# A decoder trunk on one core: the last matrix of a block ended half by half, and x transposed by VectorE and DMA

## The chip, the cores and the metric

One core of one Trainium2 chip runs the whole program in one launch. The metric is the device time of one execution in microseconds (us), and less is better. The kernel before takes 1875.56 us (median of three runs, 1875.54 to 1876.08).

The engines are named as in the profile: PE is TensorE (PEld its weight loads), DVE is VectorE, ACT is ScalarE, POOL is GpSimd, SP is SyncE, which here issues nearly all DMAs. Each engine runs its own instructions strictly in the order in which they stand.

## The reference

Four layers over 256 tokens of width 1024, all in float32. With `i` the layer and three kinds of mixer in turn:

```python
for i in range(DEPTH):                        # DEPTH = 4
    x = x + 0.5 * swiglu(rms_norm(x, norm_g[i, 0]), ffn_gate[i, 0], ffn_up[i, 0], ffn_down[i, 0])
    hn = rms_norm(x, norm_g[i, 1])
    mix = (short_conv_mixer, mla_mixer, spatial_gating_mixer)[i % 3](hn, ...)
    x = x + mix
    x = x + 0.5 * swiglu(rms_norm(x, norm_g[i, 2]), ffn_gate[i, 1], ffn_up[i, 1], ffn_down[i, 1])

def rms_norm(x, g):                           # per token
    return x * rsqrt(mean(x * x) + 1e-6) * g
def swiglu(x, w_gate, w_up, w_down):          # 1024 -> 2816 -> 1024
    return (silu(x @ w_gate) * (x @ w_up)) @ w_down
```

So there are twelve blocks in a row, three to a layer (feed-forward, mixer, feed-forward). Each one begins with the norm of x and a product that contracts over the 1024 columns of x, and ends with a product that is added to x. The mixers are a short gated convolution (layers 0 and 3), latent attention (MLA, layer 1) and a spatial gating (layer 2).

## The kernel before

**Tokens.** The 256 tokens are two tiles of 128, `x0` and `x1`, that stay on chip with the tokens in the partitions. Each goes through the twelve blocks in a stream of its own (`stream(t)`, a Python generator). A `yield` ends a *turn*; the loop at the end gives the two streams their turns alternately, and stream 0 starts four turns ahead (`LAG`). What a turn emits is appended to the engines' orders; nothing is reordered afterwards. `later(n, f)` puts work off by n turns, counted over both streams.

**Weights.** All weight matrices form one list of *units* of 1024 columns in all (two k-tiles of 512 columns, or one k-tile of 1024). SP loads a unit (512 KB) into one of six `raw` buffers, ACT rounds it to float32r (`whi`, line 102) and DVE forms the rest (`wlo`, line 109). Each unit is used by stream 0 and then, four units later, by stream 1. A left operand is split in the same way (`split`, lines 243 and 244), and `products` (lines 289, 290 and 292) makes three matmuls of a product: high by high, high by low, and, last, low by high. One turn of a large product is one unit, six matmuls of 512 columns.

**The end of a block.** `linear_rows` takes units of one k-tile with all 1024 columns and writes two PSUM banks, one for each half of the columns. Both halves end with the last k-tile. `residual` then adds both to x on DVE (lines 363 and 365), and ACT sums the squares of both halves (line 353).

**The start of a block.** `normed` transposes x, since the contraction needs the columns of x in the partitions: for each half four transposes by PE with an identity (line 251), a multiplication by the norm's gain on DVE that empties the PSUM bank (line 334), and the split. The factor of the norm is applied later, to the product. `linear` then makes one bank of 512 columns over all eight k-tiles.

**A transpose without PE is there already**, for the hidden activations of the feed-forward (`turned`): DVE transposes blocks of 32 by 32 (line 391), SP writes the tile to HBM (`turn`, line 265) and reads it back in another order with four DMAs (line 269), and ACT and DVE split what arrived (lines 275 and 276, `take`).

In the names below, h0 and h1 are the first and second half of the 1024 columns of x.

Of the kernel before, what the change touches and what calls it, by code (L numbers as in the profile page):

```python
# [24 lines left out]
P = 128  # L25
# [25 lines left out]
LAG = 4  # L51
SKEW = 2
# [10 lines left out]
class Weights:  # L63
    """The weight matrices as one stream of units in the order of their use."""
# [56 lines left out]
def trunk(ctx: ExitStack, tc: tile.TileContext, x, positions, norm_g, ffn_gate, ffn_up, ffn_down,  # L121
# [185 lines left out]
    def linear_rows(t, a, n_kt):  # L307
# [18 lines left out]
    def normed(t, i, which):  # L326
        """x * gain, transposed and split, and the factor of each token: the first turn ends before, one between."""
        g0 = (i * 3 + which) * NK
        a = []
        for h in range(2):  # L330
            yield
            tr = transposed([xs[t][:, (4 * h + k) * P : (4 * h + k + 1) * P] for k in range(4)])
            xg = slot([P, 4, P])
            nc.vector.tensor_tensor(out=xg, in0=tr, op=ALU.mult,  # L334
                                    in1=columns[0][:, g0 + 4 * h : g0 + 4 * h + 4].unsqueeze(2).broadcast_to([P, 4, P]))
            a.append(split(xg, [P, 4, P]))
        in_chain[t] = False
        yield
        r = factor(sums_of_x[t] or sum_x(t))
        sums_of_x[t] = None  # L340
        return a, r

    sums_of_x = [None] * NT

    def factor(sums):
        total = tiny(1, "total")
        nc.gpsimd.tensor_tensor(out=total, in0=sums[0], in1=sums[1], op=ALU.add)  # L347
        return power(total, EPS, 1.0 / D, 1, "rstd")
# [19 lines left out]

# [1 line left out]
    def plan_ffn(i, j):  # L370
        for c, w in FF_CHUNKS:
            for m in (ffn_gate, ffn_up):
                W.add(m[i, j], c, w, NK, UNIT // w)
        W.add(ffn_down[i, j], 0, D, DFF // P, 1)

    def ffn(t, i, j, _):
        a, r = yield from normed(t, i, 2 * j)
        hs = []
        for n, (c, w) in enumerate(FF_CHUNKS):
            gate = yield from linear(t, a, w, NK)  # L380
            sg = slot([P, w])
            nc.scalar.activation(sg, gate[:, :w], AF.Silu, scale=r)  # L382
            yield
            up = yield from linear(t, a, w, NK)
# [5 lines left out]
            nc.vector.scalar_tensor_tensor(out=h, in0=up[:, :w], scalar=r, in1=sg, op0=ALU.mult, op1=ALU.mult)  # L390
# [6 lines left out]
        ps = yield from linear_rows(t, lambda k: hs[k // 4], DFF // P)  # L397
        residual(t, ps, 0.5)

# [1 line left out]
    def plan_conv(ia):  # L401
        for j in range(2):
            for part in (1, 2, 0):
                W.add(conv_w_in[ia], part * D + j * 512, 512, NK, 2)
        W.add(conv_w_out[ia], 0, D, NK, 1)

    def conv(t, i, ia, shared):
        a, r = yield from normed(t, i, 1)
# [26 lines left out]
        for j in range(2):  # L435
            c = yield from linear(t, a, 512, NK)
            cs = slot([P, 512])
            nc.scalar.activation(cs, c, AF.Copy, scale=r)
            yield
            hp = yield from linear(t, a, 512, NK)  # L440
# [9 lines left out]
        ps = yield from linear_rows(t, lambda k: ms[k // 4], NK)  # L450
        residual(t, ps, 1.0)

# [31 lines left out]
    def spatial(t, i, ic, _):  # L484
        a, r = yield from normed(t, i, 1)
        vs, sums = [], []
        for j in range(2):
            v = yield from linear(t, a, 512, NK)
# [4 lines left out]
            yield  # L493
# [36 lines left out]
    def plan_mla(ib):  # L530
# [5 lines left out]
        W.add(mla_w_o[ib], 0, D, NK, 1)  # L536
# [4 lines left out]
    def prepare_rope():  # L541
        """cos and sin [128 tok, NT, 16] of positions * inv_freq, the angle reduced exactly."""
# [111 lines left out]
    def rope_into(dst, src, table, t, n):  # L654
        """dst, src [128, n, 32]: rotated, with the gain in the table."""
# [9 lines left out]
    def mla(t, i, ib, shared):  # L665
        a, r = yield from normed(t, i, 1)
# [26 lines left out]
        def head_squares(y, n, how):  # L693
            """The sums of squares of y[:, h, :n]."""
# [162 lines left out]
    def stream(t):  # L857
        for n, (kind, i, j) in enumerate(blocks):
# [4 lines left out]
            yield from kinds[kind][1](t, i, j, shareds[n])  # L863
        for h in range(2):
            cols = slice(h * D // 2, (h + 1) * D // 2)
            (nc.sync, nc.scalar)[h].dma_start(out=out[0, t * P : (t + 1) * P, cols], in_=xs[t][:, cols])
# [44 lines left out]
```

## Time and profile before

| what | value |
| --- | --- |
| time, median of three runs | 1875.56 us |
| span of the profiled execution, first to last instruction | 1873.2 us |
| what lies around the span (the difference of the two) | 2.4 us |
| PE busy | 1852.3 us, 99% of the span |
| DVE, ACT, POOL busy | 60%, 47%, 5% |
| mean granted TensorE clock | 0.996 of full speed |
| moved by DMA | 382 MB, 204 GB/s over the span |

The profile is of one execution, and the page gives its span. Busy time of PE counts an instruction from its start to its modelled end, and neighbours overlap; what a matmul takes of PE's time is read from the distance between the starts of two in a row. Idle time with a releaser in brackets says what an instruction waited for.

### The profile page before, as it was taken

The numbers are of one execution on the slowest core, as the hardware profiler recorded it, in microseconds if no ns is written. First come the engines' busy times: TensorE is split into PE (matmuls) and PEld (weight loads), VectorE is DVE, ScalarE is ACT, GpSimd is POOL, SyncE is SP. The second block draws the span as 40 slices with busy tenths as digits, with TensorE's granted clock in tenths as the row PEclk, the third lists the DMA queues.
The fourth block names the chain that finished last, engine by engine and source line by source line (L and its number), as shares of the span: only waits on it lengthen the run. The fifth ranks groups of instructions, "written<-read, shape, count | busy, mean of one in ns | idle before, by whom it ended". The sixth has DMA issues, their size and how long they took to land.

```text
span 1873.2 us, 23300 instructions
## 1 busy us (share of the span) xinstructions
PE 1852.3 (99%) x8654; PEld 1523.4 (81%) x8654; DVE 1119.3 (60%) x1357; ACT 879.4 (47%) x1172; POOL 88.8 (5%) x222
## 2 busy tenths in 40 slices
PE   8999999999999989999999999999999999999998
PEld 6888888888888878888888888788888888888887
DVE  6555676565656476656556555565646564765662
ACT  5444454444445376544444445454435453544452
POOL 1000000000501031000010000000000000000000
PEclk9999999999999999999999999999999999999999
DMA  7777456777577630677757774467856784556782
GB/s 261 237 243 229 156 173 192 245 241 228 168 238 246 201 108 13 201 234 231 242 188 228 230 242 157 158 199 238 267 162 206 239 269 153 190 169 213 235 267 72
DMA packets 190162, 382.42 MB, mean 204 GB/s; under 512 B 14406, under 2 KB 57568, under 8 KB 190048
## 3 DMA queue, kind: packets, MB, share of 16 engines
q1 hardware_dynamic: 189040, 379.25, 63.0%
q0 software_dynamic: 608, 1.11, 0.2%
q8 instruction: 67, 1.10, 0.2%
q10 hardware_dynamic: 400, 0.57, 0.1%
q14 instruction: 47, 0.39, 0.1%
HBM read 356.76 MB, written 24.12 MB: 203 GB/s over the span
## 4 chain that ended last, share of the span: by engine, by line
PE 96%; ACT 2%; DVE 1%; issue 0%; DMA 0%; POOL 0%; SPq 0%; ACTq 0%; DVEq 0%
PE acc L289 31%; PE acc L292 31%; PE acc L290 31%; PE tr L251 2%; PE acc L820 1%; PE acc L793 1%; ACT whi L102 0%; DVE wlo L109 0%; DMA raw<-in_ffn_gate_dram 0%; ACT s L353 0%; ACT s L718 0%; ACT s L699 0%; ACT s L750 0%; PE acc L506 0%; DVE s L334 0%
## 5 line engine op out<-in xcount | busy, mean ns | idle before, releaser
L289 PE MATMUL acc<-whi,s 128*128 128x512 f32 (+2 forms) x2664 | 1028.3, 386 | 2.6 <-ACT s L243 1.8
L290 PE MATMUL acc<-wlo,s 128*128 128x512 f32 (+2 forms) x2664 | 1019.5, 383 | 1.6 <-DVE wlo L109 1.5
L292 PE MATMUL acc<-whi,s 128*128 128x512 f32 (+2 forms) x2664 | 953.6, 383 | 0.0
L109 DVE TENSOR_TENSOR wlo<-raw,whi 128x1024 fp32r<-128x1024 f32 (+1 forms) x634 | 749.8, 1214 | 182.2 <-ACT whi L102 181.0
L102 ACT ACTIVATE whi<-raw 128x1024 fp32r<-128x1024 f32 (+1 forms) x634 | 639.5, 1048 | 223.9 <-PE acc L292 202.3
L292 PEld LDWEIGHTS acc<-whi,s 128*128 128x128 f32 x2664 | 501.1, 188 | 106.6 <-DVE s L244 1.0
L289 PEld LDWEIGHTS acc<-whi,s 128*128 128x128 f32 x2664 | 501.3, 188 | 105.6 <-ACT s L243 2.9
L290 PEld LDWEIGHTS acc<-wlo,s 128*128 128x128 f32 x2664 | 501.6, 188 | 104.4 <-DVE wlo L109 2.5
L382 ACT ACTIVATE s<-acc,rstd 128x512 f32<-128x512 f32 (+1 forms) x96 | 62.7, 653 | 456.8 <-PE acc L292 447.9
L390 DVE SCALAR_TENSOR_TENSOR s<-acc,rstd,s 128x512 f32<-128x512 f32 (+1 forms) x96 | 67.7, 705 | 230.6 <-PE acc L292 230.1
L276 DVE TENSOR_TENSOR s<-big,s 128x512 fp32r<-128x512 f32 x96 | 61.8, 644 | 128.6 <-ACT s L275 128.6
L353 ACT ACTIVATE s<-x 128x512 bf16<-128x512 f32 x52 | 32.4, 623 | 110.8 <-DVE x L365 77.6
L243 ACT ACTIVATE s<-s 128x512 fp32r<-128x512 f32 (+1 forms) x58 | 36.4, 628 | 87.3 <-DVE s L334 63.8
L347 POOL TENSOR_TENSOR total<-ss,ss 128x1 f32<-128x1 f32 x26 | 6.3, 243 | 1446.6 <-ACT s L353 1446.6
L391 DVE STREAM_TRANSPOSE big<-s 128x512 f32<-128x512 f32 (+1 forms) x96 | 64.1, 667 | 3.3
L275 ACT ACTIVATE s<-big 128x512 fp32r<-128x512 f32 x96 | 56.2, 585 | 20.2 <-DMA big<-turn 19.9
L244 DVE TENSOR_TENSOR s<-s,s 128x512 fp32r<-128x512 f32 (+1 forms) x58 | 39.9, 688 | 40.3 <-ACT s L243 40.3
L365 DVE SCALAR_TENSOR_TENSOR x<-acc,x 128x512 f32<-128x512 f32 x32 | 20.6, 686 | 68.0 <-PE acc L292 68.0
L251 PE MATMUL tr<-ident,s 128*128 128x128 f32 (+1 forms) x222 | 33.6, 281 | 9.0 <-ACT s L765 2.5
L251 PEld LDWEIGHTS tr<-ident,s 128*128 128x128 f32 (+1 forms) x222 | 26.2, 140 | 16.5 <-ACT s L765 4.3
L334 DVE TENSOR_TENSOR s<-tr,columns 128x512 f32<-128x512 f32 x48 | 32.9, 686 | 8.8 <-PE tr L251 8.8
L251 PEld LDWEIGHTS tr<-ident,x 128*128 128x128 f32 x192 | 24.6, 144 | 6.1
(121 smaller groups left out, 412.4 us busy)
## 6 DMA issues: line engine op xcount, KB each, us to landing
raw<-in_ffn_gate_dram SPq DMA_DIRECT2D x176, 512.0 KB, 4.7
raw<-in_ffn_up_dram SPq DMA_DIRECT2D x176, 512.0 KB, 5.1
raw<-in_ffn_down_dram SPq DMA_DIRECT2D x176, 512.0 KB, 4.6
raw<-in_conv_w_in_dram SPq DMA_DIRECT2D x48, 512.0 KB, 3.9
turn<-big SPq DMA_DIRECT2D x32, 512.0 KB, 3.8
big<-turn SPq DMA_DIRECT2D x128, 128.0 KB, 4.5
raw<-in_conv_w_out_dram SPq DMA_DIRECT2D x16, 512.0 KB, 4.5
raw<-in_sg_w_in_dram SPq DMA_DIRECT2D x16, 512.0 KB, 3.7
```

What stands on the lines that cost most here:

```text
L102: nc.scalar.activation(hi, src, AF.Copy)
L109: self.nc.vector.tensor_tensor(out=lo, in0=src, in1=hi.bitcast(F32), op=ALU.subtract)
L244: nc.vector.tensor_tensor(out=lo, in0=src, in1=hi.bitcast(F32), op=ALU.subtract)
L251: nc.tensor.transpose(tr[: part.shape[-1], n, :], part, ident)
L275: nc.scalar.activation(hi.rearrange("p k (i b) -> p k i b", b=32), src, AF.Copy)
L276: nc.vector.tensor_tensor(out=lo.rearrange("p k (i b) -> p k i b", b=32), in0=src, in1=hi.bitcast(F32).rearrange("p k (i b) -> p k i b", b ...
L289: nc.tensor.matmul(ps, lhsT=ah[:, k, :], rhs=wh[:, wk, c], start=first, stop=False)
L290: nc.tensor.matmul(ps, lhsT=ah[:, k, :], rhs=wl[:, wk, c], start=False, stop=False)
L292: nc.tensor.matmul(ps, lhsT=al[:, k, :], rhs=wh[:, wk, c], start=False, stop=last)
L382: nc.scalar.activation(sg, gate[:, :w], AF.Silu, scale=r)
L390: nc.vector.scalar_tensor_tensor(out=h, in0=up[:, :w], scalar=r, in1=sg, op0=ALU.mult, op1=ALU.mult)
L391: nc.vector.transpose(z[:, :, k0 : k0 + w // P].rearrange("p j k b -> p k j b"), h.rearrange("p (k j b) -> p k j b", j=4, b=32))
```

## The change

- **A block's last product ends half by half.** Its last 8 k-tiles (feed-forward, `DOWN_TAIL`) or 4 (mixers, `OUT_TAIL`) are taken as units of two k-tiles and 512 columns: first all of h0, then all of h1 (`plan_rows`, `rows_into_x`). The residual of h0 is added four units (two in the mixers) before that of h1.
- **A block's first two products are interleaved by halves of k** (`plan_pair`, `linear_pair`): both over h0 of x first, then both over h1. This holds for gate and up, for two parts of the convolution's input matrix, and for two of spatial gating's.
- **Each half of x is transposed as soon as it is added, in one of two ways** (`prepare_x`). Where the block that begins is a mixer or the first feed-forward of a layer, `by_dma` holds: DVE transposes blocks of 32 by 32 (line 409), SP writes 256 KB to HBM (line 414) and reads it back with four DMAs (line 418), ACT multiplies by the gain in four pieces (line 423), and the split follows. Where it is the second feed-forward of a layer, the transposes stay on PE (`turn_by_pe`, line 433). With 12 blocks, 7 of the 11 passages from block to block go by DMA: 28 halves over the two streams.
- **The turns without work** at a block's start are two (four for MLA), before there were three that held the transposes.
- **The output** is stored half by half, without the sums of squares that no block needs.

```diff
+DOWN_TAIL, OUT_TAIL = 8, 4
+X_TURN, X_WRITE, X_READ, X_TAKE = 2, 1, 4, 8
+IDLE_FIRST, IDLE_DMA, IDLE_PE, IDLE_MLA = 1, 2, 2, 4
...
+    def plan_rows(w, n_kt, tail):
+        W.add(w, 0, D, n_kt - tail, 1)
+        for h in range(2):
+            W.add(w, 512 * h, 512, n_kt, 2, n_kt - tail)
+    def rows_into_x(t, a, n_kt, tail, factor, then):
+        ps = [acc(), acc()]
+        cols = [slice(0, 512), slice(512, 1024)]
+        for k in range(n_kt - tail):
+            products(ps, a(k), k % 4, unit(t), 0, cols, k == 0, False)
+            yield
+        for h in range(2):
+            for k in range(n_kt - tail, n_kt, 2):
+                w = unit(t)
+                for j in range(2):
+                    products([ps[h]], a(k + j), (k + j) % 4, w, j, [cols[0]], k + j == 0, k + j == n_kt - 1)
+                if k < n_kt - 2:
+                    yield
+            residual(t, ps[h], h, factor)
+            if then is not None:
+                prepare_x(t, h, *then)
+            else:
+                (nc.sync, nc.scalar)[h].dma_start(out=out[0, t * P : (t + 1) * P, 512 * h : 512 * h + 512], in_=x_half(t, h))
+            if h == 0:
                 yield
-        return ps
+        in_chain[t] = True
...
+    def linear_pair(t, a, width, n_kt, first_done):
+        ps = [acc(), acc()]
+        for k0 in range(0, n_kt, n_kt // 2):
+            for n in range(2):
+                k = k0
+                while k < k0 + n_kt // 2:
+                    w = unit(t)
+                    for j in range(w[2]):
+                        products([ps[n][:, :width]], a[(k + j) // 4], (k + j) % 4, w, j, [slice(0, width)], k + j == 0, k + j == n_kt - 1)
...
+    def prepare_x(t, h, i, which, by_dma):
+        g = gain_at(i, which, h)
+        lhs[t][h] = None
+        later(1, lambda: square_x(t, h))
+        if not by_dma:
+            later(X_TURN, lambda: turn_by_pe(t, h, g))
+            return
+        z = slot([P, 4, 4, 32])
+        nc.vector.transpose(z.rearrange("p j k b -> p k j b"), x_half(t, h).rearrange("p (k j b) -> p k j b", j=4, b=32))
+        d = dram.tile([4, 32, 4, 4, 32], F32, tag="xturn", name=name("xturn"))
+        y = slot([P, 4, 4, 32])
+        def write():
+            nc.sync.dma_start(out=d.rearrange("i a j k b -> (i a) j k b"), in_=z)
+        def read():
+            for j in range(4):
+                nc.sync.dma_start(out=y[32 * j : 32 * j + 32], in_=d[:, :, j].rearrange("i a k b -> a i k b"))
+        def take():
+            xg = slot([P, 4, P])
+            for k in range(4):
+                nc.scalar.activation(xg[:, k, :].rearrange("p (i b) -> p i b", b=32), y[:, :, k], AF.Copy, scale=g[:, k : k + 1])
+            lhs[t][h] = split(xg, [P, 4, P])
+        later(X_WRITE, write)
+        later(X_READ, read)
+        later(X_TAKE, take)
...
+    def normed(t, idle):
+        for _ in range(idle):
+            yield
+        in_chain[t] = False
+        return Lhs(t), factor(sums_of_x[t])
...
+                then = (next_i, 2 * next_j, n % 3 != 1) if next_kind == "ffn" else (next_i, 1, True)
```

The first place is DVE at the passage from the first feed-forward to the convolution. `x0_81` and `x1_82` are the two tiles of x. Before:

```order
L109 TENSOR_TENSOR wlo67_1607<-raw67_1508,whi67_1606 128x1024
L365 SCALAR_TENSOR_TENSOR x0_81<-acc_142_1191,x0_81 128x512
L365 SCALAR_TENSOR_TENSOR x0_81<-acc_143_1192,x0_81 128x512
L109 TENSOR_TENSOR wlo68_1625<-raw68_1526,whi68_1624 128x1024
L334 TENSOR_TENSOR s_168_1655<-tr_167_1650,columns0_87 128x512
L244 TENSOR_TENSOR s_170_1658<-s_168_1655,s_169_1657 128x512
```

And in the changed kernel, from h1's neighbours on (h0 of x0 was added and transposed six rows earlier). The first `L246` is the split of x0's h0 as it came back by DMA, the second that of x1's h0, the third that of x0's h1:

```order
L394 SCALAR_TENSOR_TENSOR x1_82<-acc_157_1290,x1_82 128x512
L409 STREAM_TRANSPOSE s_177_1638<-x1_82 128x4x4x32
L246 TENSOR_TENSOR s_185_1648<-s_183_1642,s_184_1647 128x512
L394 SCALAR_TENSOR_TENSOR x0_81<-acc_147_1192,x0_81 128x512
L409 STREAM_TRANSPOSE s_189_1665<-x0_81 128x4x4x32
L111 TENSOR_TENSOR wlo68_1656<-raw68_1526,whi68_1655 128x1024
L111 TENSOR_TENSOR wlo69_1706<-raw69_1544,whi69_1705 128x1024
L246 TENSOR_TENSOR s_205_1738<-s_203_1732,s_204_1737 128x512
L111 TENSOR_TENSOR wlo70_1724<-raw70_1571,whi70_1723 128x1024
L394 SCALAR_TENSOR_TENSOR x1_82<-acc_158_1291,x1_82 128x512
L409 STREAM_TRANSPOSE s_207_1751<-x1_82 128x4x4x32
L246 TENSOR_TENSOR s_215_1761<-s_213_1755,s_214_1760 128x512
```

The split of a half that came by DMA now stands ahead of the residual of the next half, and the third split stands behind a `wlo`, a residual and a transpose.

The second place is SP at the same passage. Before, it held only weight loads here:

```order
L89 DMA raw69_1544<-in_conv_w_in_dram 128x2x512
L89 DMA raw70_1562<-in_conv_w_in_dram 128x2x512
L89 DMA raw71_1580<-in_conv_w_in_dram 128x2x512
L89 DMA raw72_1598<-in_conv_w_in_dram 128x2x512
L89 DMA raw73_1616<-in_conv_w_in_dram 128x2x512
L89 DMA raw74_1642<-in_conv_w_in_dram 128x2x512
```

In the changed kernel (`xturn_169` is x0's h0, `xturn_178` x1's h0, `xturn_190` x0's h1):

```order
L414 DMA xturn_169_1564<-s_168_1562 128x512
L91 DMA raw70_1571<-in_conv_w_in_dram 128x2x512
L91 DMA raw71_1589<-in_conv_w_in_dram 128x2x512
L418 DMA s_170_1565<-xturn_169_1564 32x4x128 x4
L91 DMA raw72_1611<-in_conv_w_in_dram 128x2x512
L91 DMA raw73_1629<-in_conv_w_in_dram 128x2x512
L414 DMA xturn_178_1640<-s_177_1638 128x512
L414 DMA xturn_190_1667<-s_189_1665 128x512
L91 DMA raw74_1674<-in_conv_w_in_dram 128x2x512
L418 DMA s_179_1641<-xturn_178_1640 32x4x128 x4
L418 DMA s_191_1668<-xturn_190_1667 32x4x128 x4
```

Two weight loads stand between the write and the reads of x0's h0, and the reads of x1's h0 stand behind the write of x0's h1.

The third place is PE at the start of MLA, whose products are 416 columns wide. Before, `s_615` is the high part of x0's h0, and units of x1's last product (`acc_599`, `acc_600`) stand between its own:

```order
L289 MATMUL acc_624_5648<-whi230_5546,s_615_5615 128x416
L290 MATMUL acc_624_5648<-wlo230_5547,s_615_5615 128x416
L292 MATMUL acc_624_5648<-whi230_5546,s_616_5616 128x416
L289 MATMUL acc_624_5648<-whi230_5546,s_615_5615 128x416
L290 MATMUL acc_624_5648<-wlo230_5547,s_615_5615 128x416
L292 MATMUL acc_624_5648<-whi230_5546,s_616_5616 128x416
L289 MATMUL acc_599_5248<-whi229_5528,s_607_5389 128x512
L290 MATMUL acc_599_5248<-wlo229_5529,s_607_5389 128x512
L289 MATMUL acc_600_5249<-whi229_5528,s_607_5389 128x512
L290 MATMUL acc_600_5249<-wlo229_5529,s_607_5389 128x512
L292 MATMUL acc_599_5248<-whi229_5528,s_608_5390 128x512
L292 MATMUL acc_600_5249<-whi229_5528,s_608_5390 128x512
```

And now, with `s_686` the high part of x0's h0 and `s_710` that of x0's h1:

```order
L291 MATMUL acc_717_5755<-whi231_5633,s_686_5661 128x416
L292 MATMUL acc_717_5755<-wlo231_5634,s_686_5661 128x416
L294 MATMUL acc_717_5755<-whi231_5633,s_687_5662 128x416
L291 MATMUL acc_717_5755<-whi232_5669,s_710_5741 128x416
L292 MATMUL acc_717_5755<-wlo232_5670,s_710_5741 128x416
L294 MATMUL acc_717_5755<-whi232_5669,s_711_5742 128x416
```

Between the first product with h0 and the first with h1 stand 12 matmuls of x0 alone; before, units of x1's last product and PE's transposes stood among them.

## Rows read from the trace of the kernel before

**Rows 1.** The page: PE's and the others' busy time, GB/s in 40 slices, the chain.
```profile
PE 1852.3 (99%) x8654; PEld 1523.4 (81%) x8654; DVE 1119.3 (60%) x1357; ACT 879.4 (47%) x1172; POOL 88.8 (5%) x222
...
GB/s 261 237 243 229 156 173 192 245 241 228 168 238 246 201 108 13 201 234 231 242 188 228 230 242 157 158 199 238 267 162 206 239 269 153 190 169 213 235 267 72
...
PE 96%; ACT 2%; DVE 1%; issue 0%; DMA 0%; POOL 0%; SPq 0%; ACTq 0%; DVEq 0%
```

**Rows 2.** PE's groups: busy us, mean ns of one, idle before, releaser.
```profile
L251 PE MATMUL tr<-ident,x 128*128 128x128 f32 x192 | 29.5, 278 | 0.0
```

**Rows 3.** PE's timeline at a passage: start us, us, instruction.
```profile
193.98 0.60 PE L251 MATMUL tr<-ident,x 128*128 128x128 f32 x4
194.33 0.48 PE L289 MATMUL acc<-whi,s 128*128 128x512 f32 x1
194.65 0.39 PE L290 MATMUL acc<-wlo,s 128*128 128x512 f32 x1
...
195.81 0.60 PE L251 MATMUL tr<-ident,x 128*128 128x128 f32 x4
```

**Rows 4.** Groups of DVE and ACT by form, columns as in rows 2.
```profile
L365 DVE SCALAR_TENSOR_TENSOR x<-acc,x 128x512 f32<-128x512 f32 x32 | 20.6, 686 | 68.0 <-PE acc L292 68.0
L391 DVE STREAM_TRANSPOSE big<-s 128x512 f32<-128x512 f32 x80 | 56.9, 712 | 2.7
L244 DVE TENSOR_TENSOR s<-s,s 128x512 fp32r<-128x512 f32 x56 | 38.8, 693 | 39.1 <-ACT s L243 39.1
L109 DVE TENSOR_TENSOR wlo<-raw,whi 128x1024 fp32r<-128x1024 f32 x626 | 742.0, 1216 | 178.4 <-ACT whi L102 177.3 <-DMA turn<-big 0.3
...
L243 ACT ACTIVATE s<-s 128x512 fp32r<-128x512 f32 x56 | 35.4, 632 | 84.9 <-DVE s L334 63.8 <-DVE s L432 21.1
L353 ACT ACTIVATE s<-s 128x128 bf16<-128x128 f32 x2 | 0.6, 293 | 0.0
```

**Rows 5.** SP's and ACT's timeline: the third turned tile of the first feed-forward.
```profile
132.47 0.33 SPq L265 DMA_DIRECT2D turn<-big  x1
133.57 1.47 SPq L89 DMA_DIRECT2D raw<-in_ffn_down_dram  x2
135.09 1.85 SPq L269 DMA_DIRECT2D big<-turn  x4
...
143.27 0.63 ACT L275 ACTIVATE s<-big 128x512 fp32r<-128x512 f32 x1 [3.32 <-DMA big<-turn]
```

**Rows 6.** The same two engines: such a tile in two later feed-forwards.
```profile
1336.49 0.33 SPq L265 DMA_DIRECT2D turn<-big  x1
...
1345.17 0.63 ACT L275 ACTIVATE s<-big 128x512 fp32r<-128x512 f32 x1 [1.19 <-DMA big<-turn]
...
1802.40 0.33 SPq L265 DMA_DIRECT2D turn<-big  x1
...
1813.49 0.64 ACT L275 ACTIVATE s<-big 128x512 fp32r<-128x512 f32 x1 [3.61 <-DMA big<-turn]
```

**Rows 7.** DMA issues: count, KB each, median us from issue to landing.
```profile
out_dram<-x SPq DMA_DIRECT2D x2, 256.0 KB, 2.1
```

**Rows 8.** PE in MLA: timeline; then stretches (us, busy, clock, DMA share, GB/s).
```profile
671.33 0.35 PE L290 MATMUL acc<-wlo,s 128*128 128x416 f32 x1
671.52 0.35 PE L292 MATMUL acc<-whi,s 128*128 128x416 f32 x1
673.98 0.55 PE L251 MATMUL tr<-ident,s 128*128 128x128 f32 x3 [2.11 <-ACT s L669]
...
675.00:680.00 5.00, 4.70 (x23) 1.00 0.74 226
685.00:690.00 5.00, 5.00 (x27) 0.77 0.03 12
```

**Rows 9.** The whole timeline at the very end.
```profile
1868.17 1.29 DVE L365 SCALAR_TENSOR_TENSOR x<-acc,x 128x512 f32<-128x512 f32 x2 [4.25 <-PE acc L292]
...
1869.49 0.34 ACTq L866 DMA_DIRECT2D out_dram<-x  x1
```

More of the change, by code (lines that the diff above doesn't have):

```diff
@@ L324, in power @@
         return r
[L326 to L348, printed above, removed]
+    lhs = [[None, None] for _ in range(NT)]
+    sums_of_x = [[None, None] for _ in range(NT)]
     def square_sum(src):
@@ L370, in plan_ffn, with square_x, factor @@
[L370 to L377, printed above, removed]
+    def square_x(t, h):
+        sums_of_x[t][h] = square_sum(x_half(t, h))
+    def factor(sums):
+        total = tiny(1, "total")
+        nc.gpsimd.tensor_tensor(out=total, in0=sums[0], in1=sums[1], op=ALU.add)
+        return power(total, EPS, 1.0 / D, 1, "rstd")
@@ new lines, in x_half, with residual, gain_at @@
+    def x_half(t, h):
+        return xs[t][:, h * 512 : (h + 1) * 512]
+    def residual(t, ps, h, factor):
+        part = x_half(t, h)
+        if factor == 1.0:
+            nc.vector.tensor_tensor(out=part, in0=ps, in1=part, op=ALU.add)
+        else:
+            nc.vector.scalar_tensor_tensor(out=part, in0=ps, scalar=factor, in1=part, op0=ALU.mult, op1=ALU.add)
+    def gain_at(i, which, h):
+        g0 = (i * 3 + which) * NK + 4 * h
+        return columns[0][:, g0 : g0 + 4]
+    def prepare_x(t, h, i, which, by_dma):
[22 more added lines that the diff above has]
+        later(X_TAKE, take)
@@ new lines, in turn_by_pe, with __init__, __getitem__ @@
+    def turn_by_pe(t, h, g):
+        tr = transposed([xs[t][:, (4 * h + k) * P : (4 * h + k + 1) * P] for k in range(4)])
+        xg = slot([P, 4, P])
+        nc.vector.tensor_tensor(out=xg, in0=tr, op=ALU.mult, in1=g.unsqueeze(2).broadcast_to([P, 4, P]))
+        lhs[t][h] = split(xg, [P, 4, P])
+    class Lhs:
+        def __init__(self, t):
+            self.t = t
+        def __getitem__(self, h):
+            assert lhs[self.t][h] is not None, (self.t, h)
+            return lhs[self.t][h]
@@ L378, in ffn, with gate_done @@
+    def ffn(t, i, j, _, then):
+        a, r = yield from normed(t, IDLE_FIRST if i + j == 0 else (IDLE_DMA, IDLE_PE)[j])
         hs = []
+        sg = [None]
+        def gate_done(ps, w):
+            sg[0] = slot([P, w])
+            nc.scalar.activation(sg[0], ps[:, :w], AF.Silu, scale=r)
         for n, (c, w) in enumerate(FF_CHUNKS):
[L380 to L383, printed above, removed]
@@ L396, in ffn, with conv @@
             yield
-        ps = yield from linear_rows(t, lambda k: hs[k // 4], DFF // P)
-        residual(t, ps, 0.5)
+        yield from rows_into_x(t, lambda k: hs[k // 4], DFF // P, DOWN_TAIL, 0.5, then)
     def plan_conv(ia):
         for j in range(2):
-            for part in (1, 2, 0):
+            if j == 0:
+                plan_pair(conv_w_in[ia], conv_w_in[ia], D, 2 * D, 512, NK)
+            for part in (1, 2, 0)[2 - 2 * j :]:
                 W.add(conv_w_in[ia], part * D + j * 512, 512, NK, 2)
-        W.add(conv_w_out[ia], 0, D, NK, 1)
-    def conv(t, i, ia, shared):
-        a, r = yield from normed(t, i, 1)
+        plan_rows(conv_w_out[ia], NK, OUT_TAIL)
+    def conv(t, i, ia, shared, then):
+        a, r = yield from normed(t, IDLE_DMA)
         ms = [None] * 2
@@ L449, in conv @@
             yield
-        ps = yield from linear_rows(t, lambda k: ms[k // 4], NK)
-        residual(t, ps, 1.0)
+        yield from rows_into_x(t, lambda k: ms[k // 4], NK, OUT_TAIL, 1.0, then)
     def plan_spatial(ic):
-        for c in (D, D + 512, 0, 512):
+        plan_pair(sg_w_in[ic], sg_w_in[ic], D, D + 512, 512, NK)
+        for c in (0, 512):
             W.add(sg_w_in[ic], c, 512, NK, 2)
-        W.add(sg_w_out[ic], 0, D, NK, 1)
+        plan_rows(sg_w_out[ic], NK, OUT_TAIL)
     sg_wT = [fixed([P, 4, P], f"sg_wT{j}") for j in range(2)]
@@ L482, in prepare_spatial, with spatial, v_done @@
         later(70, load)
-    def spatial(t, i, ic, _):
-        a, r = yield from normed(t, i, 1)
+    def spatial(t, i, ic, _, then):
+        a, r = yield from normed(t, IDLE_DMA)
         vs, sums = [], []
-        for j in range(2):
-            v = yield from linear(t, a, 512, NK)
+        def v_done(v):
             vv = slot([P, 512])
@@ L525, in spatial @@
             yield
-        ps = yield from linear_rows(t, lambda k: ms[k // 4], NK)
-        residual(t, ps, 1.0)
+        yield from rows_into_x(t, lambda k: ms[k // 4], NK, OUT_TAIL, 1.0, then)
     def plan_mla(ib):
@@ L839, in mla @@
             yield
-        ps = yield from linear_rows(t, lambda k: os_[k // 4], NK)
-        residual(t, ps, 1.0)
+        yield from rows_into_x(t, lambda k: os_[k // 4], NK, OUT_TAIL, 1.0, then)
     kinds = {"ffn": (plan_ffn, ffn, None), "conv": (plan_conv, conv, None), "mla": (plan_mla, mla, prepare_mla),
@@ L857, in stream @@
     def stream(t):
+        for h in range(2):
+            yield
+            turn_by_pe(t, h, gain_at(0, 0, h))
+            later(1, lambda h=h: square_x(t, h))
         for n, (kind, i, j) in enumerate(blocks):
@@ L862, in stream @@
                     prepare(blocks[n + 1][2])
[L863 to L866, printed above, removed]
+            then = None
+            if n + 1 < len(blocks):
+                next_kind, next_i, next_j = blocks[n + 1]
+                then = (next_i, 2 * next_j, n % 3 != 1) if next_kind == "ffn" else (next_i, 1, True)
+            yield from kinds[kind][1](t, i, j, shareds[n], then)
     with tc.manual_schedule(engines=MANUAL):
```

65 lines of the change are left out of this document (38 added, 27 removed).

## The prediction

> **What bounds the kernel now.** The page first [rows 1]: PE is busy 99% of the span and makes 96% of the chain that ended last; DVE, ACT and the DMA engines have slack. So only what PE runs and what PE waits for counts. Then PE's groups [rows 2]: the 192 transposes of x never left PE idle, so the old start of a block hides its chain and there is nothing to win there but PE's own time. PE's timeline gives the prices [rows 3]: the last five matmuls of 512 columns of a unit take 1.16 us (194.65 to 195.81), 0.232 us each, so a unit of six takes 1.39 us. PE's longest waits, the 2.1 us at 673.98 among them, lie in MLA [rows 8].
>
> **PE loses transposes.** Four of them take 0.35 us (193.98 to 194.33), and the matmul behind them is followed after 0.32 instead of 0.23 us (194.33 to 194.65): 0.44 us for a group [rows 3]. 28 halves go by DMA now: 28 x 0.44 = 12.3 us less on PE, all of it on the path. The matmuls of the tails and the pairs are the same as before in number and width, so PE's other work is unchanged.
>
> **The end.** Now two residuals (1.29 us) stand between the last matmul and the last store [rows 9]; then one does. 0.6 us less.
>
> **The way by DMA, one half (x0's h0).** I count from the end of the last matmul of that half. DVE starts after 0.1 us; residual 0.69, transpose 0.71 [rows 4]: the write is issued at 1.5. For the DMAs the trace has the same pattern on SP, write, two weight loads, four reads: from 132.47 to 143.27 the third tile of the first feed-forward took 10.8 us until ACT, which stood waiting for it, could start [rows 5]. There are eight such tiles; they took 8.7 (the quickest) to 11.1 us, 9.8 in the mean [rows 6]. They hold 384 KB, x's half 256 KB: 0.25 MB less in all at some 240 GB/s [rows 1] is 1.0 us, so 8.8 us. The bounds: two transfers as quick as a lone store of 256 KB, 2.1 us each [rows 7], and 1.4 us to issue three reads ahead of the fourth [rows 5], 5.6 us; above, the slowest tile as it is, 11.1. I take 8.8, since the neighbours on the queue are the same. The data are there at 10.3. Then ACT's four pieces, 4 x 0.29 = 1.2, high part 0.63, low part 0.69 [rows 4]: high at 12.1, low at 12.8 (9.6 to 15.1).
>
> The Trainium skill prices this lower: "DMA: Bandwidth & Descriptors", section "Anatomy of one DMA", gives about 2.0 us for each DMA whatever its size, plus its bytes. By it an estimate for write and reads is 2.6 + 2.6 us and the issue of the reads, 6.6 us in all. The lone store of 256 KB at 2.1 us agrees with it [rows 7]; the loaded queue, with 8.7 to 11.1 us, does not [rows 6], and the trace decides. What it would give is the first rival.
>
> **What hides it.** PE reaches x0's h0 ten units later, at 13.9 us: hidden. But each engine works in its own order. On DVE the split of h0 stands ahead of the residual of x0's h1, whose last matmul ends at 11.1 (eight units). So that residual starts at 12.8 instead of 11.2, and the write of h1 is issued at 14.2. On SP the reads of x1's h0 stand behind that write: 1.1 us for the write, 0.4 for a load [rows 5], then two times four reads, 15.7 to 17.5 and 17.5 to 19.4. In rows 5 and 6 all reads had landed 5.2 to 8.5 us (mean 7.1) after the first was issued; here 0.6 MB less stands ahead, 2.3 us less: 4.8. So x1's h0 lands at 20.5, x0's h1 a quarter of a megabyte later, at 21.5. ACT splits the one (high at 22.3) and then the other (high at 24.1). DVE: low part of x1's h0 at 23.0, then `wlo` 1.22, the residual of x1's h1 and its transpose, 1.40, and only then the low part of x0's h1, at 26.3. PE wants x0's h1 nine units after its last matmul, at 23.6, and its low part two matmuls later, at 24.1. Stall: 2.2 us. With the quick bound the delay on DVE goes and the stall is 0; with the slow one it is about 4.5. x1's h1 has ten units and the stall before it: hidden. There are six such passages (two into the convolution, three into a layer's first feed-forward, one into spatial gating): 6 x 2.2 = 13.2 us, between 0 and 27.
>
> **MLA.** Here the first product is not a pair. x0's h0 is wanted after twelve units: hidden. x0's h1 is wanted 12 matmuls of 416 columns later, 0.19 us each [rows 8], at 16.7 + 2.3 = 19.0, its low part at 19.4. By the steps above its high part is there at 24.1, and the low one at 25.1 (no `wlo` stands before it here): 5.7 us of stall, 3.0 with the quick bound. x1's h1 is added on DVE at 23.7, written at 24.4, landed by 30.4 and split by 32.2 and 32.9, while PE, which resumed at 25.1, wants it at 29.7: 2.8 more. Before, PE stood 2.1 us at this place for the evacuation of x0's product [rows 8]; now units of x1 cover that: 2.1 back. x0's next split stands on ACT behind this `take`: some 1.5 us (between 0 and 3). 5.7 + 2.8 - 2.1 + 1.5 = 7.9 us, between 1 and 11.
>
> **Edits at nothing.** The four passages to a layer's second feed-forward keep PE's transposes one unit after the residual, as before, which cost PE no wait [rows 2]; if the residual came later than 1.39 us, PE would wait for the rest. ACT gets 28 x 1.2 = 33 us more, at 47% busy; where it blocks on a landing, `whi` made three units ahead covers it, and the price without that cover is the wait itself. SP blocks on a write's landing before its reads, as it does now for every turned tile; weights have six buffers ahead of it, 6 x 2 x 1.39 = 16.7 us, and if these ran out PE would wait for `whi`. 14.7 MB more on the queues is 4% of 382 MB. The paired products fill two banks instead of one for two units; six banks are there.
>
> **Sum.** The profiled execution's span is 1873.2 us, with 2.4 us around it that stay: the median, 1875.6. -12.3 - 0.6 + 13.2 + 7.9 = +8.2: 1883.8 us.
>
> **Rivals.** *All hidden but MLA.* If a half's DMAs take 7 us or less, the split of h0 is done when h1's last matmul is, nothing cascades, and the six passages cost 0. For it: a lone store takes 2.1 us [rows 7], and a half of x is smaller than any turned tile. Against it: eight waits for such reads out of eight, with the same neighbours on the queue [rows 5, 6]. With MLA at 4: -12.9 + 4 = 1866.7 us, faster. *Halfway.* DMAs a microsecond shorter than mine, stalls of 1 us: -12.9 + 6 + 6, 1874.7 us, no change. *The clock falls.* In MLA a wait of 2.1 us alone [rows 8] left the granted clock at 1.00 (675 to 680); after further waits it was 0.77 over 5 us (685 to 690), a mix of 2.4 and 1.2 GHz, which loses 1.15 us. If each of the seven passages brought that, 8 us more than the forecast: 1892 us. The place is the first units of a block, the price 1.15 us each, and it decides where two stalls come within a few units. The Trainium skill ("TensorE: Matmul & The Clock Gate", section "HAM oscillation — how this bites in real kernels") has this rule: waits for DMA between bursts of matmuls bring the clock to its lower level again and again. The trace has it for MLA only.
>
> **Chances.** Forecast, slower: 0.42 (0.05 of it so near that nothing can be told). All hidden: 0.33, of which 0.02 within the bound. Halfway: 0.15, of which 0.03 faster and 0.12 no change. The clock: 0.10, slower. A measurement of this kernel tells 0.2%, 3.75 us. So faster 0.34, no change 0.19, slower 0.47. The forecast's own range is 1877 to 1891 (stalls of 1 to 3.5 us in the six); with the cases of the other sign 1863 (nothing waits but MLA's three microseconds) to 1897 (stalls of 3.5 us and the clock).
>
> **What would show it.** PE's transposes of x: 80 instead of 192. In PE's idle time, some 2 us at the first product with x0's h1 in six passages, released by ACT or DVE line 246 (not by the weights), and 5 us or more in MLA. On DVE, line 394 for h1 held behind line 246 although PE is done; on ACT, line 423 waiting for `xturn`'s reads. Wrong would be: no wait of PE on line 246 outside MLA, or reads that land within 7 us of their write. If PE waits on `whi` or `wlo` instead, the queue on SP or a blocked ACT is the cost, which I put at nothing.

## The result: 1898.8 us, 1.3% slower

The changed kernel takes 1898.84 us (median of four runs, 1896.66 to 1905.40) against 1875.71; the ratio is 1.013, 95% interval [1.0112, 1.0147]. The forecast was slower, by 8.2 us; it became 23.1, 2 us above the top of the range. The profile is of the quickest of the four runs.

The page of the kernel after (its span is 1894.9 us), with the groups that answer to [rows 1, 2]:

```profile
PE 1851.4 (98%) x8542; PEld 1512.8 (80%) x8542; DVE 1118.0 (59%) x1357; ACT 908.4 (48%) x1276; POOL 114.7 (6%) x222
PE 88%; DMA 4%; ACT 3%; DVE 3%; SPq 1%; issue 1%; ACTq 0%; DVEq 0%
L291 PE MATMUL acc<-whi,s 128*128 128x512 f32 (+1 forms) x2664 | 1029.8, 387 | 20.2 <-ACT s L245 19.3
L294 PE MATMUL acc<-whi,s 128*128 128x512 f32 (+1 forms) x2664 | 982.0, 384 | 7.4 <-DVE s L246 7.3
L423 ACT ACTIVATE s<-s,columns 128x128 f32<-128x128 f32 x112 | 35.8, 390 | 94.0 <-DMA s<-xturn 94.0
...
L253 PE MATMUL tr<-ident,x 128*128 128x128 f32 x80 | 13.4, 297 | 0.0
```

80 transposes of x are left on PE instead of 192, as forecast. But PE's share of the chain that ended last fell from 96% to 88%, and DMA, ACT and DVE stand in it. PE waits 19.3 us for high parts of x (ACT, line 245) and 7.3 us for low parts (DVE, line 246).

The idle time in these two rows, 27.6 us, is not all that was lost: PE's busy time has hardly fallen (1852.3 to 1851.4) though 12.3 us of transposes are gone. PE's timeline at the passage from the first feed-forward into the convolution shows why (start, duration, idle before and releaser), beside [rows 3]:

```profile
202.98 0.39 PE L294 MATMUL acc<-whi,s 128*128 128x512 f32 x1
204.57 0.50 PE L291 MATMUL acc<-whi,s 128*128 128x512 f32 x1 [1.20 <-ACT s L245]
204.91 0.40 PE L292 MATMUL acc<-wlo,s 128*128 128x512 f32 x1
205.30 0.50 PE L294 MATMUL acc<-whi,s 128*128 128x512 f32 x1
205.64 0.40 PE L291 MATMUL acc<-whi,s 128*128 128x512 f32 x1
...
206.41 0.50 PE L291 MATMUL acc<-whi,s 128*128 128x512 f32 x1
206.74 0.40 PE L292 MATMUL acc<-wlo,s 128*128 128x512 f32 x1
208.35 0.50 PE L294 MATMUL acc<-whi,s 128*128 128x512 f32 x1 [1.21 <-DVE s L246]
208.69 0.39 PE L291 MATMUL acc<-whi,s 128*128 128x512 f32 x1
```

From 202.98 to 208.69 there are ten starts, which take 2.32 us at 0.232; they take 5.71, so 3.4 us are lost, and the brackets show 2.4. Matmuls overlap, so a wait begins to cost 0.16 us before it counts as idle; and a matmul that had to wait is followed after 0.34 instead of 0.23 us, which happens twice for a half, since its high part comes first and its low part just behind it (205.30). From here on losses are taken from starts. Summed so, the six passages lose 3.4, 3.3, 8.6, 3.7, 3.1 and 2.5 us: 24.5 in all, where the forecast had 13.2.

What PE waits for stands on the other three engines (the same passage, from the residual of x0's h0 on):

```profile
181.15 0.69 DVE L394 SCALAR_TENSOR_TENSOR x<-acc,x 128x512 f32<-128x512 f32 x1 [7.41 <-PE acc L294]
...
182.61 0.34 SPq L414 DMA_DIRECT2D xturn<-s  x1
...
185.31 1.84 SPq L418 DMA_DIRECT2D s<-xturn  x4
...
192.00 1.31 ACT L423 ACTIVATE s<-s,columns 128x128 f32<-128x128 f32 x4 [6.56 <-DMA s<-xturn]
192.36 4.06 SPq L414 DMA_DIRECT2D xturn<-s  x2
193.34 0.63 ACT L245 ACTIVATE s<-s 128x512 fp32r<-128x512 f32 x1
194.01 0.69 DVE L246 TENSOR_TENSOR s<-s,s 128x512 fp32r<-128x512 f32 x1 [1.67 <-ACT s L245]
194.62 0.68 DVE L394 SCALAR_TENSOR_TENSOR x<-acc,x 128x512 f32<-128x512 f32 x1
197.66 3.97 SPq L418 DMA_DIRECT2D s<-xturn  x8
202.58 1.28 ACT L423 ACTIVATE s<-s,columns 128x128 f32<-128x128 f32 x4 [4.53 <-DMA s<-xturn]
203.89 0.63 ACT L245 ACTIVATE s<-s 128x512 fp32r<-128x512 f32 x1
...
204.42 1.26 ACT L423 ACTIVATE s<-s,columns 128x128 f32<-128x128 f32 x4
...
205.72 0.63 ACT L245 ACTIVATE s<-s 128x512 fp32r<-128x512 f32 x1
206.30 0.68 DVE L394 SCALAR_TENSOR_TENSOR x<-acc,x 128x512 f32<-128x512 f32 x1
...
207.65 0.65 DVE L246 TENSOR_TENSOR s<-s,s 128x512 fp32r<-128x512 f32 x1
```

The residual of x0's h1 (194.62) follows the split of x0's h0 without a gap, 2.3 us after it could have run (the end of h0's last matmul is put at 181.05, 0.1 us ahead of its residual; that of h1 ends eight units, 11.1 us, later, and DVE follows after 0.1); its write on SP (the second of the two, done at 196.42) is as late; the eight reads for two halves then go out together, and ACT takes both halves back to back (202.58, 204.42). The low part of x0's h1 (207.65) stands behind a weight's low part, the residual of x1's h1 and its transpose.

### The profile page after: what moved, and what is told of

Same layout as the page of the kernel before. It is cut to its first block, busy times and chain, and to the rows that moved or that the text cites. A ratio compares the mean times of both kernels' runs of the same rounds, so it can differ in the third digit from the quotient of the medians.

```text
span 1894.9 us, 23349 instructions
## 1 busy us (share of the span) xinstructions
PE 1851.4 (98%) x8542; PEld 1512.8 (80%) x8542; DVE 1118.0 (59%) x1357; ACT 908.4 (48%) x1276; POOL 114.7 (6%) x222
## 4 chain that ended last, share of the span: by engine, by line
PE 88%; DMA 4%; ACT 3%; DVE 3%; SPq 1%; issue 1%; ACTq 0%; DVEq 0%
PE acc L294 28%; PE acc L291 28%; PE acc L292 28%; DMA s<-xturn 3%; PE tr L253 2%; DVE wlo L111 1%; ACT s L423 1%; SPq L418 1%; ACT s L245 1%; DVE s L246 1%; DMA xturn<-s 1%; PE acc L919 1%; PE acc L892 1%; DVE x L394 0%; ACT whi L104 0%
## 5 line engine op out<-in xcount | busy, mean ns | idle before, releaser
L291 PE MATMUL acc<-whi,s 128*128 128x512 f32 (+1 forms) x2664 | 1029.8, 387 | 20.2 <-ACT s L245 19.3
L292 PE MATMUL acc<-wlo,s 128*128 128x512 f32 (+1 forms) x2664 | 1022.2, 384 | 1.5 <-DVE wlo L111 1.5
L294 PE MATMUL acc<-whi,s 128*128 128x512 f32 (+1 forms) x2664 | 982.0, 384 | 7.4 <-DVE s L246 7.3
L246 DVE TENSOR_TENSOR s<-s,s 128x512 fp32r<-128x512 f32 (+1 forms) x58 | 39.6, 683 | 114.7 <-ACT s L245 114.7
L383 POOL TENSOR_TENSOR total<-ss,ss 128x1 f32<-128x1 f32 x26 | 14.1, 542 | 1449.5 <-ACT s L375 1449.5
L423 ACT ACTIVATE s<-s,columns 128x128 f32<-128x128 f32 x112 | 35.8, 390 | 94.0 <-DMA s<-xturn 94.0
L520 DVE SCALAR_TENSOR_TENSOR s<-s,columns,s 128x128 f32<-128x128 f32 x64 | 22.5, 352 | 2.3
```

## The experiments

Each ratio is to the kernel before, run beside the variant. A1 is the theory that what costs is not the transfer but what stands in order behind an instruction that waits for its landing.

**1. All halves by PE**, ends by halves and pairs kept:

```
-  then = (next_i, 2 * next_j, n % 3 != 1) if next_kind == "ffn" else (next_i, 1, True)
+  then = (next_i, 2 * next_j, False) if next_kind == "ffn" else (next_i, 1, False)
```

> The changed kernel with every half of x turned by PE again (192 transposes of x); the ends by column halves and the pairs stay. Theory A (the loss is PE waiting for the DMA-turned halves): nothing waits, and only the shorter end is left of the change, 1875 us (1873 to 1877), ratio to the kernel before about 1.000. Rival B (finishing by halves and pairing the first products costs PE time by itself, since PE's recorded busy time fell by 0.9 us where 12.3 us of transposes went): the 11 us stay, 1885 us or more.

Measured 1873.33 us, ratio 0.9988 [0.9979, 0.9997]. Rival B falls: the new order of products costs nothing and is worth some 1.8 us (0.6 to 3.9 by the interval). All the loss lies in the DMA way.

**2. The take one unit later.**

```
-X_TURN, X_WRITE, X_READ, X_TAKE = 2, 1, 4, 8
+X_TURN, X_WRITE, X_READ, X_TAKE = 2, 1, 4, 9
```

> The changed kernel with X_TAKE = 9 for 8: on DVE the residual of x0's h1 comes ahead of the split of x0's h0, which waits for a landing; all DMAs are the same. Theory A1 (the landing is late by a microsecond, and the queue on DVE passes that on): x0's h1 leaves 2.3 us earlier, x1's h0 and x0's h1 land as much earlier, the six passages lose 0 to 1 us instead of 3.4 and MLA some 4.5 instead of 7: 1880 us (1876 to 1884). Rival C (the DMA round trip itself is what PE waits for, whoever stands ahead on DVE): unchanged, 1896 to 1900 us, with 3 us of wait in each passage.

Measured 1886.79 us, 1.0058 [1.0043, 1.0073]. 12 us came back with the same DMAs in the program, so C falls as it stood; but A1 had hoped for 19, and the time lies 3 us above its window. PE's timeline, the first passage:

```profile
203.92 0.50 PE L291 MATMUL acc<-whi,s 128*128 128x512 f32 x1 [0.74 <-ACT s L245]
206.37 0.50 PE L291 MATMUL acc<-whi,s 128*128 128x512 f32 x1 [0.52 <-ACT s L245]
```

The wait for a low part is gone (in the changed kernel 1.21 at 208.35), that for x1's h0 is shorter (0.74 for 1.20), x0's h1 is now waited for at its high part (0.52), and each wait still brings its two slow restarts. MLA's wait fell only from 7.08 to 6.36. Of the 10.0 us between the two profiled executions 6.0 lie at the one passage behind the sixth block, which loses 2.6 instead of 8.6 us. The other five lose 14.1 us where they lost 15.9, so there most of what C said holds: ACT takes x1's h0 0.1 us after it has landed (201.82).

**3. MLA by PE.**

```
-  ... else (next_i, 1, True)
+  ... else (next_i, 1, next_kind != "mla")
```

> The changed kernel with the four halves into MLA turned by PE, the rest by DMA as they were. Theory A: MLA's entry costs 7.7 us of the difference; PE's 7 us wait at its first product goes, the 2 us wait of before for the evacuation may come back: 1891 us (1889 to 1893). Rival (the waits in MLA are covered by the later waits of that block, which would move up): 1896 us or more.

Measured 1888.92 us, 1.0072 [1.0056, 1.0089]: 9.9 us back by the medians, 8.2 between the profiled executions; the trace of the changed kernel has 7.2 for MLA (below).

**4. Both edits**, those of 2 and 3 together.

> X_TAKE = 9 and MLA's halves by PE. Theory A1: both savings add, 1874 us (1871 to 1878). Rival C: as the variant with MLA alone, 1889 to 1893 us.

Measured 1881.33 us, 1.0033 [1.0022, 1.0044]: 5.5 us under the second, 7.6 under the third. That misses A1's window by 3 us, and so does not beat PE's transposes: a passage saves 4 x 0.44 = 1.8 us and loses 2.9 in the mean (2.6 in the first one, where 0.9 shows as idle). A half that comes just in time is still too late.

**5 to 8. A longer tail**, so that h0 ends 5.6 us earlier (two units of its own stream and two of the other's). It stands on top of the fourth; then on top of the second, with h0 alone by DMA (the second pair of lines); on top of the third; and on top of the first.

```
-DOWN_TAIL, OUT_TAIL = 8, 4
+DOWN_TAIL, OUT_TAIL = 12, 4
...
-        if not by_dma:
+        if h == 1 or not by_dma:
```

> The variant with X_TAKE = 9 and MLA's halves by PE, and DOWN_TAIL = 12 for 8: the first column half ends six units before the stream's end instead of four, so x0's h0 and x1's h0 have 5.6 us more of other units between their end and their use, x's second halves as much as before (12.5 and 13.9 us). Theory A1 (two halves of a chunk that come together meet in the queues of DVE, ACT and SP, and each arrives some tenths to 3 us late): the first halves are hidden and far from the second ones, only x0's h1 can be late, by 0 to 0.9 us a passage: 1866 us (1862 to 1870). Rival D (each half's way takes as long as its cover whatever is around it, and every half that arrives just in time costs a restart of some 0.4 us): at most the two first halves' share of the loss goes, 1873 us or more.

> DOWN_TAIL = 12, X_TAKE = 9, and of every passage that goes by DMA in the changed kernel (MLA too) only h0 does, h1 is turned by PE: 14 halves by DMA, each with 5.6 us more cover. Theory A1: nothing is late, and 14 x 0.44 = 6.2 us come off the variant with all halves by PE (1873.3): 1867 us (1865 to 1870). Rival D (the removed transposes are not worth 0.44 us each, since PE's recorded busy time did not fall): 1873 us.

> DOWN_TAIL = 12 and MLA's halves by PE, but X_TAKE = 8 as in the changed kernel. With the longer tail the split of x0's h0 is no longer just ahead of the residual of x0's h1 on DVE. Theory A1: the place of the take matters only by what is queued behind it, so this is as the variant with X_TAKE = 9, within 2 us of it. Rival: an early take blocks ACT and DVE whatever stands behind, 3 us or more above it.

> All halves by PE and DOWN_TAIL = 12: the control for the longer tail. By every theory as with DOWN_TAIL = 8: 1873 us (1871 to 1875); if the longer tail had a price of its own (512-column slices of the weights, two units more of single-bank products), some us more.

Measured 1878.58 (1.0017 [1.0007, 1.0026]), 1878.15 (1.0014 [1.0004, 1.0023]), 1872.20 (0.9982 [0.9973, 0.9992]) and 1872.72 (0.9986 [0.9976, 0.9995]). The eighth, the control, is as expected. The fifth and the sixth missed A1's windows; the fifth fits rival D, the sixth is 5 us worse than D too. The seventh beat the fifth by 6.4 us, although only the take moved, and there A1 (no difference) and its rival (the early take is the dearer one) both missed. The longer tail alone, with the take at 8 and MLA by PE (1888.92 to 1872.20), gave 16.7 us, so a half's cover counts as well as its place in the order; with the take at 9 it gave 2.8. In the fifth, x0's h1 had landed at 202.80, and ACT, whose take stood a unit later, had not to wait for it but came too late for PE; in the seventh ACT stood waiting, and PE waited less (the first two lines are of the fifth, the others of the seventh):

```profile
204.13 1.26 ACT L423 ACTIVATE s<-s,columns 128x128 f32<-128x128 f32 x4
206.10 0.50 PE L291 MATMUL acc<-whi,s 128*128 128x512 f32 x1 [1.38 <-ACT s L245]
...
203.57 1.28 ACT L423 ACTIVATE s<-s,columns 128x128 f32<-128x128 f32 x4 [1.74 <-DMA s<-xturn]
205.57 0.50 PE L291 MATMUL acc<-whi,s 128*128 128x512 f32 x1 [0.56 <-ACT s L245]
```

A take can also stand too early. The timeline of the sixth (h0 alone) shows it:

```profile
198.53 1.28 ACT L423 ACTIVATE s<-s,columns 128x128 f32<-128x128 f32 x4 [2.93 <-DMA s<-xturn]
200.38 2.00 ACT L104 ACTIVATE whi<-raw 128x1024 fp32r<-128x1024 f32 x2
200.51 0.69 DVE L246 TENSOR_TENSOR s<-s,s 128x512 fp32r<-128x512 f32 x1 [4.18 <-ACT s L245]
201.46 2.36 DVE L111 TENSOR_TENSOR wlo<-raw,whi 128x1024 fp32r<-128x1024 f32 x2 [0.26 <-ACT whi L104]
203.74 0.69 DVE L394 SCALAR_TENSOR_TENSOR x<-acc,x 128x512 f32<-128x512 f32 x1
204.48 0.82 PE L253 MATMUL tr<-ident,x 128*128 128x128 f32 x4 [1.99 <-DVE x L394]
```

PE does not need x1's h0 for a long time yet. But its take blocks ACT, the weights' high parts come late, DVE makes two low parts in a row, and the residual of x1's h1, which was turned by PE and touches no DMA, comes late: PE waits for that.

**9. The sixth, taken at 11** instead of 9, one constant:

```
-X_TURN, X_WRITE, X_READ, X_TAKE = 2, 1, 4, 9
+X_TURN, X_WRITE, X_READ, X_TAKE = 2, 1, 4, 11
```

> As the variant with DOWN_TAIL = 12 and h0 alone by DMA (1878 us), but X_TAKE = 11 for 9: the same DMAs, only the place on ACT and DVE where the landed half is taken is two units later, still three units ahead of its use. In that variant ACT stood 2.9 us at the take of x1's h0, the next weights' high and low parts and the residual of x1's h1 stood behind it, and PE waited 2.0 us for that residual. Theory A1 (what costs is what is queued behind a take that waits for its landing): nothing waits any more, and 14 x 0.44 = 6.2 us come off the variant with all halves by PE (1873): 1867 us (1865 to 1870). Rival D (the transposes removed are worth nothing, or the DMAs take the time elsewhere): 1873 us or more.

Measured 1865.33 us, 0.9946 [0.9930, 0.9963]: 12.8 us under the sixth and 7.4 under the control, where 14 x 0.44 = 6.2 were due. The timeline at the same place:

```profile
196.29 1.26 ACT L423 ACTIVATE s<-s,columns 128x128 f32<-128x128 f32 x4
...
201.05 0.69 DVE L394 SCALAR_TENSOR_TENSOR x<-acc,x 128x512 f32<-128x512 f32 x1 [0.62 <-PE acc L294]
...
202.24 0.60 PE L253 MATMUL tr<-ident,x 128*128 128x128 f32 x4
```

No engine waits for the landing, DVE waits for PE again, and PE's transposes run without idle time. D falls: a transpose taken off PE is worth its price.

**10. Both halves by DMA**, h0 taken after 11 units, h1 after 8, into MLA h0 alone; `DOWN_TAIL` is 12, `X_TAKE` 8.

```
-                prepare_x(t, h, *then)
+                prepare_x(t, h, *then[:2], then[2] and not (then[1] == 1 and then[0] == 1 and h == 1))
...
-        later(X_TAKE, take)
+        later((11, X_TAKE)[h], take)
```

> DOWN_TAIL = 12, both halves by DMA as in the changed kernel (into MLA h0 alone), h0 taken after 11 units, h1 after 8. Theory A1: the fourteen h0 halves are free (6.2 us), x0's h1 stays at the edge of its 12.5 us of cover, 0.5 to 1 us a passage against 0.88 saved there, the passage behind the sixth block some 3 us worse: 1867 us (1863 to 1871). Rival D: 1873 us or more.

Measured 1862.80 us, 0.9932 [0.9917, 0.9947], 0.2 us under A1's window and better than both kernels. ACT still stands 29.2 us for landings, in its group's row, and PE hardly notices:

```profile
L291 PE MATMUL acc<-whi,s 128*128 128x512 f32 (+1 forms) x2664 | 1027.5, 386 | 2.4 <-ACT s L245 1.2 <-ACT whi L104 1.0
L423 ACT ACTIVATE s<-s,columns 128x128 f32<-128x128 f32 x104 | 33.0, 389 | 29.4 <-DMA s<-xturn 29.2
```

**11 and 12. The write on ACT's DMA queue**, in the changed kernel and in the tenth.

```
-            nc.sync.dma_start(out=d.rearrange("i a j k b -> (i a) j k b"), in_=z)
+            nc.scalar.dma_start(out=d.rearrange("i a j k b -> (i a) j k b"), in_=z)
```

> The changed kernel, with the write of each x half issued on ACT's DMA queue instead of SP's; reads stay on SP. In the changed kernel a write landed 2.8 to 5.1 us after its issue, with weight loads issued ahead of it on the same queue, and a lone store of the same size took 2.1 us. Theory E (the write waits behind the weight loads of its own queue): it lands in some 2 to 2.6 us, each half comes about 1.5 us earlier, the first wait of each passage goes and the second shrinks: 1886 us (1880 to 1890). Rival F (the DMA engines are shared, so the queue of issue does not matter): 1897 us (1894 to 1900), or more where ACT now stands for the transpose ahead of the write.

> The variant with h0 taken after 11 units and h1 after 8, with the write on ACT's DMA queue. Theory E: x0's h1 is hidden as well, 1863 us (1861 to 1866). Rival F: as without it, 1867 us, or some us more where ACT stands for the transpose.

Measured 1903.62 us (1.0148 [1.0133, 1.0164]) and 1862.50 (0.9928 [0.9913, 0.9943]). E's premise was a misreading: 2.8 and 5.1 us are waits of SP for a landing, while the writes of the changed kernel landed a median of 2.1 us after their issue, as the lone store did; from ACT's queue it is 2.0. Mainly x1's h0 gained, 2.0 to 2.5 us where five of its seven writes had taken 3.0 to 3.4. And in the changed kernel its write now stood behind ACT's wait for x0's h0:

```profile
192.74 1.28 ACT L423 ACTIVATE s<-s,columns 128x128 f32<-128x128 f32 x4 [7.25 <-DMA s<-xturn]
...
194.12 0.33 ACTq L414 DMA_DIRECT2D xturn<-s  x1
```

It was issued at 194.12, and from SP at 192.36: A1 once more. In the tenth variant, where the order no longer blocks, it made no difference.

## Why the prediction was wrong

**Transposes, 12.3 us less.** Right: 80 are left, and experiment 9 got 7.4 us for half of them.

**The end, 0.6 us less.** Small, but under-sized: 1.2 in the trace (last residual at 1891.09 of 1894.9; before at 1868.17 of 1873.2) [rows 9].

**The way of one half.** This length, from which the stalls were worked out, was mis-sized. The steps came in the order foretold, each later. Counted from 181.05:

| step | forecast | measured |
|---|---|---|
| write issued | 1.5 | 1.6 |
| ACT takes it | 10.3 | 10.95 |
| low part | 12.8 | 13.65 |
| residual of x0's h1 starts | 12.8 | 13.6 |
| x1's h0, high part | 22.3 | 23.5 |
| x0's h1, high part | 24.1 | 25.3 |
| x0's h1, low part | 26.3 | 27.25 |

From the write to the take I put 8.8 us; at the seven passages it was 9.4, 9.2, 10.6 (MLA), 9.6, 9.5, 9.1 and 8.7. I had taken the mean of eight turned tiles and subtracted a microsecond for the smaller size [rows 5, 6]; that discount was mostly not there. The Trainium skill's price ("DMA: Bandwidth & Descriptors", section "Anatomy of one DMA"), by which the estimate was 6.6 us, was further off; that section fits it to DMAs issued by GpSimd, and SP issued these. What took long were the reads: the write of x0's h0 landed after 2.0 us in all seven passages, the last of its four reads 4.3 to 6.4 us after its issue, with two weight loads issued ahead of it.

**The six passages, 13.2 us.** Here the sum failed, at 24.5, and the step that failed is x1's h0, which was put at nothing without a reason. The prediction foretold its high part for 22.3 and its low part for 23.0 and never set them against PE's need, which is 22.2 and 22.6 (PE was ready at 203.2). Every passage waits there, and with the restarts these waits cost 10.0 us. At x0's h1, where all 13.2 us were forecast, the loss is 10.0 as well. The last 4.6 us were lost in one passage, behind the sixth block, at x1's h1, which I had called hidden.

The cascade that was described is there (line 246 ahead of line 394 on DVE, the reads together on SP, the low part of x0's h1 last). Experiment 2, which moves the split behind the residual, shows what it is worth: 12 us, but half of that in the passage behind the sixth block. In the other five most of the loss stayed, and it went with more cover (third to seventh variant, 16.7 us) and the right place of the take (ninth and tenth). The late half:

```profile
977.00 0.34 SPq L414 DMA_DIRECT2D xturn<-s  x1
982.49 1.75 SPq L418 DMA_DIRECT2D s<-xturn  x4
...
987.97 1.28 ACT L423 ACTIVATE s<-s,columns 128x128 f32<-128x128 f32 x4 [5.60 <-DMA s<-xturn]
...
989.96 0.80 PE L291 MATMUL acc<-whi,s 128*128 128x512 f32 x1 [2.80 <-ACT s L245]
990.55 0.63 PE L292 MATMUL acc<-wlo,s 128*128 128x512 f32 x1
990.98 0.63 PE L294 MATMUL acc<-whi,s 128*128 128x512 f32 x1
```

SP stood 5.1 us for the landing of this one write, against 2.8 in the first passage. The DMA records of the trace suggest why. One packet of 16 KB, of the queue that loads instructions, ran from 979.14 to 981.00. All but seven of the write's packets had started by 979.6; these seven started one after another from 980.99 on, when that packet had ended. The DMA view of 979 to 982.4 has it (queue, packets, MB, share of the 16 engines):

```profile
q8 instruction: 1, 0.02, 3.4%
```

That the seven stood behind it on one DMA engine is inferred from the times, since the records name no engine, and whether every run has this meeting is not shown. After PE's 2.8 us wait the granted clock was at the lower of its two levels (1.2 of 2.4 GHz), matmuls came 0.43 us apart, and the wait cost 4.6 us. So the rival of the falling clock came true in this passage, and in MLA; in the stretches of the other five (200 to 212, for one) the granted clock was 1.00.

**MLA, 7.9 us.** The total is close, and by luck. Against the kernel before, PE's work behind MLA's start is 7.2 us later than its work ahead of it; with the 1.8 of its four groups of transposes, which stand in another term, that is 9.0. But the terms (5.7 + 2.8 + 1.5 - 2.1) did not come so. The first wait, for x0's h1, cost 7.3 us instead of 5.7, with a way of 10.6 instead of 8.8 us. Behind it the granted clock was at its lower level, matmuls of 416 columns came 0.35 us apart instead of 0.19, and that cost some 2.3 us, which stood in no term. x1's h1, put at 2.8, was hardly waited for (685.49); its reads landed 5.5 us after the write's issue. x0's next split (1.5) was waited for 1.20 us, at 688.44, and the wait of before at 673.98 [rows 8] is gone, as forecast. The columns of the stretch are PE, PEld, DVE, ACT, POOL, then clock, DMA share and GB/s:

```profile
677.75 0.71 PE L291 MATMUL acc<-whi,s 128*128 128x416 f32 x1 [7.08 <-ACT s L245]
...
685.49 0.46 PE L291 MATMUL acc<-whi,s 128*128 128x416 f32 x1 [0.26 <-ACT s L245]
...
688.44 0.50 PE L291 MATMUL acc<-whi,s 128*128 128x512 f32 x1 [1.20 <-ACT s L245]
```

```profile
677.00:682.00 5.00, 4.25 (x12) 3.71 (x13) 3.65 (x5) 3.96 (x7) 0.94 (x3) 0.50 0.23 79
```

**Edits at nothing.** PE's waits for `wlo` and `whi` stayed at 2.3 us, so this held in the changed kernel. Experiment 6 shows that it held by luck: with the take elsewhere, a blocked ACT was the cost, through the weights and a residual.

**The sum and the range.** -12.3 - 1.2 + 24.5 + 9.0 = +20.0, against 21.7 between the two spans; the other 1.7 us lie between the passages, in steps of up to 1.1 us, and stay open. My own bounds allowed it (-12.9 + 27 + 11 = +25.1, 1900.7 us); the range stopped at 1897 because it let the passages and MLA not be late together. They share one cause, the length of the way, and so they were. The rival with all hidden, which had a third of the chances, needed a way of 7 us; x0's h0 took 8.6 to 10.5 us from the write's issue to its landing in all seven passages, and only x1's h1 came in about 7 or less, in five.

## What to carry to other kernels

A transfer is hidden only if everything queued in order behind the instruction that takes it is hidden too: give it cover first, then place the take behind the landing but some units ahead of its reader (in the ninth variant three), and look at what stands behind it on its engine and on the engines that this one feeds. Set every arrival against its need, those that look safe too. A chain that ends within a microsecond of its need is not hidden: count it as a wait, with the restarts. And where several terms of a sum rest on one uncertain length, let them err together in the range.

## What was not expected of the hardware

A wait of PE costs more than its recorded idle time: 3.4 us lost in starts for 2.4 us shown, in the first passage. The wait for a landing on ACT cost nothing of itself (29.2 us of it in the tenth variant) and up to 12.8 us by its place (sixth against ninth). The Trainium skill says in passing ("PSUM — Partial Sum Buffer", section "Engine vs sequencer instructions") that the queues of ScalarE and VectorE are strictly first in, first out; the timelines shown here agree, and this pair of runs has its price. The queue from which a write was issued hardly changed its landing (medians of 2.1 and 2.0 us).
